# ReLU and squares of an MLP on ScalarE, four weight splits on VectorE, a bias page and later transposes

## The chip, the cores and the metric

The kernel runs on one core of one Trainium2 chip. The metric is the device time of one execution in microseconds, as the median over several runs. The profiled execution is a single one, and the durations below are from it.

## The reference

One encoder block: RMSNorm, one input projection, two groups of attention heads (A with a sliding window, ALiBi distance and sinks, B with a chunk band and relative positions), an output projection, then a squared-ReLU MLP, all in float32 on 1024 tokens of width 1024 with an inner width of 4096. What the change touches:

```python
scores = scores - slopes[:, :, None, None] * dist        # group A: slope 2^-(h+1) times |distance|
...
n2 = rms_norm(h, norm2_g[layer])
u = jnp.square(jax.nn.relu(jnp.einsum('bsd,df->bsf', n2, w_ff1[layer])))
h = h + jnp.einsum('bsf,fd->bsd', u, w_ff2[layer])
return rms_norm(h, final_norm_g)
```

## The kernel before

Every float32 operand of a large product is split into a high part (rounded to the matmul's operand type, a ScalarE copy) and a low part (`split_l`, L135: full minus high, on VectorE or GpSimd), and `mm3` (L129) issues three matmuls: high by high, high by low, low by high.

The work goes in stages: projections and attention of group A (pairs A0 to A3 of heads), of group B, the output projection (`out_proj_b`, tiles `op_B`, eight blocks of 128 tokens, `tb` 0 to 7), the first MLP product, the second one, the final norm. Both MLP products use a Strassen form: a 2 by 2 block product with seven products, numbered p = 1, 5, 6, 3, 7, 2, 4 in the order of execution. For each of eight column blocks n of the first product, `product1(n, p)` runs 24 matmuls into a PSUM tile `f1`. Its left operands `X{p}` come from the normalised tokens: transposes `tp` on TensorE, then copies (`F`) and sums (`S`) in `second_half` and `combined`, then split (`operand`, L848 and L135). Its weights: the blocks `w1` are loaded, combined into `T{n}_{p}` (VectorE, L902), split into `W{n}_{p}0` (high, ScalarE, L924) and `W{n}_{p}1` (low, L135, GpSimd before). `prepare1(n, p, at)` does that for the product at place `at` of `order1`, which begins (0,1), (0,2), (1,1), (0,5), (0,6), (0,3), (0,7), (1,5), (0,4).

After products 1, 5 and 6 ScalarE copies the PSUM tile into `kept` (`k`, L967). After 3, 7, 2 and 4 the result is complete but for a sum: `v` or `k` becomes the squared ReLU of PSUM plus the kept tile (L971 to L977), and is written to memory (`ud`) for the second product. After p = 4, four sums (L983 to L989) make the combined operands of the second product.

For the attention scores of group A, `exponentials` (L400) adds a bias to the scores, on VectorE, and takes the row minimum `nm`. The bias is the distance table `dist` times a power of two, made on GpSimd (L430) after a DMA (L429) at the first use of a pair of heads.

What sets the order: TensorE's instructions are issued in the order of the code. On the other engines a scheduler, which plays the program through, orders the instructions; each engine then works through its own list in that order and waits where an operand is late. DMAs are issued from SyncE's list (SP). `turns` holds pieces of work that `product1` and `out_proj_b` run between their matmuls, one entry at a time; an entry of `steps()` without work is an empty place. Tiles called `page` come from a pool of 35 buffers, `tst` from one of two, the PSUM tiles of the MLP from one of three.

Of the kernel before, what the change touches and what calls it, by code (L numbers as in the profile page):

```python
# [8 lines left out]
F32 = mybir.dt.float32  # L9
F32R = mybir.dt.float32r  # L10
AF = mybir.ActivationFunctionType
ALU = mybir.AluOpType
# [3 lines left out]
P = 128  # L16
# [29 lines left out]
def kernel(  # L46
# [26 lines left out]
    nc = tc.nc  # L73
# [10 lines left out]
    def page(shape, name, dt=F32R):  # L84
        return main.tile(shape, dt, tag="pg", bufs=NPAGES, name=name)
# [23 lines left out]
    def load(dst, src, mark=False):  # L109

        ins = nc.sync.dma_start(dst, src)
        if last_load[0] is not None:
            dep = mybir.DependencyInfo(mybir.DependencyClass.NoSync, mybir.DependencyReason.DATA)
            tc.add_manual_dep(ins.ins, last_load[0], dep, reason="program order")
        if mark:
            last_load[0] = ins.ins.name
# [17 lines left out]
    def split_l(engine, lo, full, hi):  # L134
        engine.tensor_tensor(lo, full, f(hi), ALU.subtract)  # L135

    def rstd(ss, n, width, name, r=None):

        if r is None:
            r = small.tile([P, width], F32, tag=f"rs{width}", name=f"r_{name}")  # L140
        u = small.tile([P, width], F32, tag=f"ru{width}", bufs=2, name=f"u_{name}")
        w = small.tile([P, width], F32, tag=f"rw{width}", bufs=2, name=f"w_{name}")
        q = small.tile([P, width], F32, tag=f"rq{width}", bufs=2, name=f"q_{name}")
        nc.scalar.activation(u, ss, AF.Sqrt, bias=eps4, scale=1.0 / (4 * n))
        nc.vector.tensor_scalar(w, ss, 1.0 / (4 * n), EPS / 4, ALU.mult, ALU.add)
        nc.vector.reciprocal(q, u)
        if width == 1:
            nc.vector.tensor_scalar(w, w, q, u, ALU.mult, ALU.add)
        else:
            nc.vector.tensor_tensor(w, w, q, ALU.mult)  # L150
            nc.vector.tensor_tensor(w, w, u, ALU.add)
        nc.vector.reciprocal(r, w)
        return r
# [51 lines left out]
    def load_xT(t, k):  # L205
        if k % 2 == 0:
            xs[t] = sp.tile([P, 2, HALF], F32, tag="xs", bufs=6, name=f"xs{t}{k // 2}")
        src = xs[t][:, k % 2]
        nc.sync.dma_start(src, xT_src[:, k, t * HALF : (t + 1) * HALF])
        gain = g1c[:, k : k + 1]  # L210
        hi, lo = (nT[t][hl][k // 2][:, k % 2] for hl in range(2))
        nc.scalar.activation(hi, src, AF.Copy, scale=gain)
        nc.vector.scalar_tensor_tensor(lo, src, gain, f(hi), ALU.mult, ALU.subtract)

    def token_scales(t):

        ss = small.tile([P, 4], F32, tag="ss4", name=f"ss1_{t}")
        for b in range(4):
            tb = 4 * t + b
            xr = sp.tile([P, D], F32, tag="xr", bufs=4, name=f"xr{tb}")  # L220
            load(xr, x[tb * P : (tb + 1) * P, :], True)
            nc.scalar.activation(xr, xr, AF.Square, accum_out=ss[:, b : b + 1])
        rstd(ss, D, 4, f"n1_{t}", r1[:, 4 * t : 4 * t + 4])
# [83 lines left out]
    dve, pool = nc.vector, nc.gpsimd  # L307
# [16 lines left out]
    for k in range(NK):  # L324
        load_xT(1, k)
    token_scales(1)
    load(psink, sinks.partition_broadcast(P))
    load(ogc, og)

# [33 lines left out]
    at = ap_.enter_context(tc.tile_pool(name="at", bufs=1, reuse_waits="tile"))  # L363
# [49 lines left out]
    class Pair:  # L413
# [5 lines left out]
            self.bias, self.out = [], {}  # L419

        def biases(self):
            if self.bias:
                return self.bias
            for s in range(2):
                h = 2 * self.j + s
                b = at.tile([P, 5 * P], F32, tag="bias", bufs=2, name=f"b_{self.kind}{h}")
                if self.kind == "A":
                    far = b[:, 2 * P : 4 * P]
                    nc.sync.dma_start(far, dist)  # L429
                    nc.gpsimd.tensor_scalar(b[:, : 2 * P], far, 2.0 ** -(h + 1), None, ALU.mult)  # L430
                else:
                    nc.sync.dma_start(b, relb[h])
                    nc.gpsimd.memset(b[:HD, 5 * P - HD :], NEG)
                    nc.gpsimd.memset(b[HD:, :HD], NEG)
                self.bias.append(b)
            return self.bias
# [219 lines left out]
    class Filler:  # L656
# [24 lines left out]
        def steps(self, n):  # L681
            self.due += n
            while self.due >= 1:
                self.due -= 1
                self.step()
# [90 lines left out]
    def flat(t):  # L776
        return t.rearrange("p a b -> p (a b)")
# [4 lines left out]
    def tst(shape, name):  # L782
        return main.tile(shape, F32, tag="tst", bufs=2, name=name)

    def pair_psum(name):
        return mps.tile([P, 2, HALF], F32, tag="ab", bufs=3, name=name)
# [94 lines left out]
    def steps(*works):  # L881
        turns.append([lambda f=f, a=a: f(*a) for f, *a in works])

    chores = {(0, 1): ((6, 0),), (0, 2): ((5, 1), (6, 1)), (1, 1): ((3, 0), (3, 1)), (0, 5): ((7, 0), (7, 1)), (0, 6): ((4, 0), (4, 1))}

# [34 lines left out]
    def split(full, name, engine, alloc):  # L922
        w = [alloc(f"{name}{hl}", hl) for hl in range(2)]
        nc.scalar.activation(w[0], full, AF.Copy)  # L924
        split_l(engine, w[1], full, w[0])
        return w

    wops, wsum = {}, {}

    def prepare1(n, p, at):  # L930
        if n >= NQ or (n, p) in wops:
            return
        made = wsum.setdefault(n, {})
        second = page2 if at < 2 or at > 4 else page1
        t = second_operands(
            lambda i, j: w1s[n, i, j], made, p, f"T{n}_{p}", dve, lambda name: second([P, 4, 2 * P], name)
        )
        wops[n, p] = split(t, f"W{n}_{p}", pool, lambda name, hl: (second if hl else page1)([P, 4, 2 * P], name, F32R))

    chains = {}  # L940

    def product1(n, p):
        a, c = chains.setdefault(n, [None, None])
        if p in (1, 5, 2):
            ps = pair_psum(f"f1_{n}_{p}")
            if p == 1:
                chains[n][0] = ps
            if p == 5:
                chains[n][1] = ps
        else:  # L950
            ps = c if p == 3 else a
        hi, lo = wops.pop((n, p))
        for u in range(2):
            cols = slice(u * P, (u + 1) * P)
            for k in range(4):
                x2 = [X[p][hl][k // 2][:, k % 2] for hl in range(2)]
                mm3(ps[:, u], (hi[:, k, cols], lo[:, k, cols]), x2, k == 0 and p in (1, 5, 2), k == 3, True)
                if k % 2:
                    turn()
        kept = saved.setdefault(n, {})  # L960
        ps = flat(ps)
        if p in (1, 5, 6):
            if p == 5 and n:
                kept[p] = tst([P, 2 * HALF], f"k{n}_{p}")
            else:
                kept[p] = page2([P, 2 * HALF], f"k{n}_{p}")
            nc.scalar.activation(kept[p], ps, AF.Copy)  # L967
            return
        v = tst([P, 2 * HALF], f"v{n}") if p == 4 else kept[{3: 6, 7: 5, 2: 1}[p]]
        if p == 7 or (n, p) == (0, 2):  # L970
            dve.tensor_tensor(v, ps, v, ALU.add)  # L971
            dve.scalar_tensor_tensor(v, v, 0.0, v, ALU.max, ALU.mult)
        else:
            if p != 4:
                dve.tensor_tensor(ps, ps, v, ALU.add)
            nc.scalar.activation(v, ps, AF.Relu)
            dve.tensor_tensor(v, ps, v, ALU.mult)  # L977
        if p != 4:
            put(n, {3: 2, 7: 4, 2: 1}[p], v)
            return  # L980

        u00, u01, u11, u10 = kept[1], kept[6], kept[5], v
        dve.tensor_tensor(u11, u10, u11, ALU.add)  # L983
        put(n, 5, u11)
        dve.tensor_tensor(u10, u00, u10, ALU.subtract)
        put(n, 7, u10)
        dve.tensor_tensor(u00, u11, u00, ALU.subtract)
        put(n, 6, u00)
        dve.tensor_tensor(u01, u01, u00, ALU.subtract)  # L989
        put(n, 3, u01)  # L990
# [17 lines left out]
    for tb in range(2, TB):  # L1008
        if tb in (3, 5):
            for d in range(2):  # L1010
                for g in range(2):
                    steps((first_half, d, tb // 4, g))
        if tb == 7:
            for g in range(2):
                steps((second_half, 0, g))
                steps()
        out_proj_b(tb, range(4))
        rows2(tb)
        if tb in (4, 5):
            prepare1(0, tb - 3, tb - 4)  # L1020
        if tb == 5:
            load1(1, ((0, 0),))
# [177 lines left out]
    g, p, n0 = order2[-GQ]  # L1200
# [57 lines left out]
```

## Time and profile before

| | us |
|---|---|
| median of 3 runs (lowest to highest) | 1082.0 (1081.73 to 1082.46) |
| profiled execution, its own time | 1082.73 |
| span of its profile | 1081.0 |
| TensorE busy | 1051.4 (97%) |
| VectorE busy | 754.9 (70%) |
| ScalarE busy | 535.9 (50%) |
| GpSimd busy | 436.7 (40%) |
| mean granted TensorE clock | 0.997 |

The page gives the busy time of each engine over the span. PE is TensorE's matmuls, PEld its weight loads, DVE is VectorE, ACT ScalarE, POOL GpSimd, SP SyncE. In rows of groups or of the timeline, `out<-in` names the tiles, the text behind it the shape, and what stands in brackets at the end is the idle time of the engine just before and the instruction that ended it. Buffer numbers are left out, so `W<-T,W` stands for any weight's split.

### The profile page before, as it was taken

The numbers are of one execution on the slowest core, as the hardware profiler recorded it, in microseconds if no ns is written. First come the engines' busy times: TensorE is split into PE (matmuls) and PEld (weight loads), VectorE is DVE, ScalarE is ACT, GpSimd is POOL, SyncE is SP. The second block draws the span as 40 slices with busy tenths as digits, with TensorE's granted clock in tenths as the row PEclk, the third lists the DMA queues.
The fourth block names the chain that finished last, engine by engine and source line by source line (L and its number), as shares of the span: only waits on it lengthen the run. The fifth ranks groups of instructions, "written<-read, shape, count | busy, mean of one in ns | idle before, by whom it ended". The sixth has DMA issues, their size and how long they took to land.

```text
span 1081.0 us, 14384 instructions
## 1 busy us (share of the span) xinstructions
PE 1051.4 (97%) x5040; PEld 873.0 (81%) x5040; DVE 754.9 (70%) x1162; ACT 535.9 (50%) x953; POOL 436.7 (40%) x320
## 2 busy tenths in 40 slices
PE   7999999999999999998999999999999999999997
PEld 6787878888888888877888888888788888888885
DVE  4577787667676765697755655656989776778667
ACT  7676765666574566654333333334423333333346
POOL 1376664343370243338453454445105024024025
PEclk9999999999999999999999999999999999999999
DMA  9945626353575342213454344516998535533004
GB/s 325 259 120 143 155 73 171 99 140 101 134 249 199 138 156 98 106 52 116 175 176 175 128 146 156 179 75 233 326 400 287 173 118 174 175 117 98 1 1 156
DMA packets 90584, 170.30 MB, mean 158 GB/s; under 512 B 7824, under 2 KB 43664, under 8 KB 90512
## 3 DMA queue, kind: packets, MB, share of 16 engines
q1 hardware_dynamic: 90368, 169.38, 47.6%
q8 instruction: 40, 0.66, 0.3%
q14 instruction: 32, 0.26, 0.1%
q10 hardware_dynamic: 144, 0.00, 0.0%
HBM read 105.39 MB, written 45.09 MB: 139 GB/s over the span
## 4 chain that ended last, share of the span: by engine, by line
PE 85%; DVE 7%; ACT 3%; issue 2%; DMA 2%; POOL 1%; SPq 1%; DVEq 0%; ACTq 0%
PE f L129 24%; PE f_a L129 16%; PE f_c L129 8%; PE op_B L129 4%; PE f_b L129 4%; PE op_A L129 4%; PE ip_qB L129 4%; PE ip_vB L129 3%; PE ip_kB L129 3%; PE av_B L129 3%; PE ip_qA L129 3%; PE S_B L129 2%; PE pt_B L132 2%; PE S_A L129 1%; PE av_A L129 1%
## 5 line engine op out<-in xcount | busy, mean ns | idle before, releaser
L129 PE MATMUL f<-X,W 128*128 128x512 f32 x1344 | 308.4, 391 | 6.5 <-POOL W L135 5.3
L129 PEld LDWEIGHTS f<-X,W 128*128 128x128 f32 x1344 | 252.9, 189 | 61.1 <-POOL W L135 6.1
L129 PE MATMUL f_a<-V,U 128*128 128x512 f32 x768 | 176.3, 389 | 0.7 <-DVE k L977 0.7
L135 POOL TENSOR_TENSOR U<-u,U 128x1024 fp32r<-128x1024 f32 x32 | 81.2, 2536 | 228.0 <-PE f_c L129 135.9
L129 PEld LDWEIGHTS f_a<-V,U 128*128 128x128 f32 x768 | 144.1, 188 | 31.0 <-issue 1.1
L135 POOL TENSOR_TENSOR W<-T,W 128x1024 fp32r<-128x1024 f32 x32 | 91.3, 2858 | 126.5 <-ACT W L924 126.5
L129 PE MATMUL f_c<-V,U 128*128 128x512 f32 x384 | 88.4, 389 | 0.0
L129 PEld LDWEIGHTS f_c<-V,U 128*128 128x128 f32 x384 | 72.1, 188 | 15.0
L924 ACT ACTIVATE V<-Z 128x1024 fp32r<-128x1024 f32 x32 | 33.9, 1060 | 94.6 <-PE f_a L129 44.6
L135 POOL TENSOR_TENSOR W<-w,W 128x1024 fp32r<-128x1024 f32 x24 | 61.0, 2544 | 35.1 <-ACT W L924 34.1
L135 DVE TENSOR_TENSOR V<-w,V 128x1024 fp32r<-128x1024 f32 x24 | 52.0, 2166 | 30.7 <-ACT V L924 30.2
L924 ACT ACTIVATE V<-w 128x1024 fp32r<-128x1024 f32 x24 | 25.4, 1059 | 81.2 <-issue 34.2
L924 ACT ACTIVATE U<-u 128x1024 fp32r<-128x1024 f32 x56 | 58.5, 1045 | 13.3 <-DVE Z L902 8.3
L924 ACT ACTIVATE W<-T 128x1024 fp32r<-128x1024 f32 x32 | 33.9, 1060 | 55.4 <-DVE T L902 28.6
L967 ACT ACTIVATE k<-f 128x1024 f32<-128x1024 f32 x24 | 24.6, 1026 | 65.6 <-PE f L129 65.6
L401 ACT ACTIVATE P_B<-P_B,nm_B 128x640 f32<-128x640 f32 (+2 forms) x64 | 44.3, 693 | 24.4 <-DVE nm_B L400 12.7
L129 PE MATMUL ip_kB<-nT,w_kB 128*128 128x512 f32 x192 | 51.5, 397 | 1.5 <-DVE T_A L135 0.8
L129 PE MATMUL op_A<-w_o,y 128*128 128x512 f32 x192 | 52.1, 397 | 0.5 <-DVE h L719 0.5
L135 DVE TENSOR_TENSOR V<-Z,V 128x1024 fp32r<-128x1024 f32 x32 | 46.3, 1448 | 8.4 <-ACT V L924 5.9
L129 PE MATMUL ip_vB<-nT,w_vB 128*128 128x512 f32 x192 | 51.9, 398 | 0.0
L129 PE MATMUL ip_qB<-nT,w_qB 128*128 128x512 f32 x192 | 51.5, 396 | 0.0
L135 DVE TENSOR_TENSOR T_B<-pt_B,T_B 128x512 fp32r<-128x512 f32 (+2 forms) x72 | 39.7, 552 | 16.7 <-ACT T_B L408 16.3
(211 smaller groups left out, 2024.7 us busy)
## 6 DMA issues: line engine op xcount, KB each, us to landing
w<-in_w_ff_dram SPq DMA_DIRECT2D x64, 512.0 KB, 4.7
u<-ud SPq DMA_DIRECT2D x56, 512.0 KB, 4.5
ud<-k SPq DMA_DIRECT2D x48, 512.0 KB, 3.0
KkB<-ts_kB SPq DMA_DIRECT2D x64, 128.0 KB, 2.3
yd<-y SPq DMA_DIRECT2D x14, 512.0 KB, 2.9
y<-yd SPq DMA_DIRECT2D x14, 512.0 KB, 6.4
xs<-in_xT_dram SPq DMA_DIRECT2D x16, 256.0 KB, 5.5
xr<-in_x_dram SPq DMA_DIRECT2D x8, 512.0 KB, 7.3
```

The source lines that it names most:

```text
L129: pe(nc.tensor.matmul(*args, **kw))
L132: pe(nc.tensor.transpose(*args))
L135: engine.tensor_tensor(lo, full, f(hi), ALU.subtract)
L401: nc.scalar.activation(pr[:, :n], pr[:, :n], AF.Exp, bias=nm, scale=-1.0, accum_out=sm)
L924: nc.scalar.activation(w[0], full, AF.Copy)
L967: nc.scalar.activation(kept[p], ps, AF.Copy)
```

## The change

It has four parts.

1. The two biases of the pair A0 are made in a page of their own, `b_A0`: one DMA of `dist` and two multiplies on GpSimd, written in the code ahead of the projections' steps. `Pair.biases` returns these for the pair A0.
2. The low parts of the weights at places 3 to 6 of `order1`, (0,5), (0,6), (0,3) and (0,7), are made on VectorE.
3. After products 3, 7 and 2, VectorE only adds PSUM and the kept tile into the kept tile; ScalarE does the ReLU and the square in place. After p = 4 ScalarE does the ReLU out of PSUM and the square in place.
4. At `tb` 7 the empty place comes ahead of `second_half`, so its transposes come one step of the output projection later.

```diff
@@ after token_scales(1)
+    fb = page([P, 3, 2 * P], "b_A0", F32)
+    load(fb[:, 2], dist)
+    first_bias = [fb[:, s] for s in range(2)]
+    for s in range(2):
+        pool.tensor_scalar(fb[:, s], fb[:, 2], 2.0 ** -(s + 1), None, ALU.mult)
     load(psink, sinks.partition_broadcast(P))
@@ Pair.biases
+            if self.kind == "A" and self.j == 0:
+                return first_bias
             if self.bias:
                 return self.bias
@@ prepare1
-        wops[n, p] = split(t, f"W{n}_{p}", pool, lambda name, hl: (second if hl else page1)([P, 4, 2 * P], name, F32R))
+        wops[n, p] = split(t, f"W{n}_{p}", dve if 2 < at < 7 else pool, lambda name, hl: (second if hl else page1)([P, 4, 2 * P], name, F32R))
@@ product1
-        if p == 7 or (n, p) == (0, 2):
+        if p == 4:
+            nc.scalar.activation(v, ps, AF.Relu)
+        else:
             dve.tensor_tensor(v, ps, v, ALU.add)
-            dve.scalar_tensor_tensor(v, v, 0.0, v, ALU.max, ALU.mult)
-        else:
-            if p != 4:
-                dve.tensor_tensor(ps, ps, v, ALU.add)
-            nc.scalar.activation(v, ps, AF.Relu)
-            dve.tensor_tensor(v, ps, v, ALU.mult)
+            nc.scalar.activation(v, v, AF.Relu)
+        nc.scalar.activation(v, v, AF.Square)
@@ tb == 7
             for g in range(2):
+                steps()
                 steps((second_half, 0, g))
-                steps()
```

The order on GpSimd at the start. Before, ahead of the first attention unit (`w1_vA`, `w1_qA1`, `w1_qA2` are low parts of projection weights, `P_A0` the normed exponentials of the first unit):

```order
L135 TENSOR_TENSOR w1_vA_239<-st_vA_237,w0_vA_238 128x256 x4
L135 TENSOR_TENSOR w1_qA1_476<-st_qA1_474,w0_qA1_475 128x256 x4
L367 MEMSET padF0_550 128x2x128
L369 MEMSET padL0_551 128x2x128
L369 MEMSET padL1_552 128x2x128
L430 TENSOR_SCALAR b_A0_568<-b_A0_568 128x256
L430 TENSOR_SCALAR b_A1_571<-b_A1_571 128x256
L135 TENSOR_TENSOR w1_qA2_580<-st_qA2_578,w0_qA2_579 128x256 x4
L505 TENSOR_SCALAR P_A0_0_0_563<-P_A0_0_0_563,rc_A0_0_561 128x256
```

GpSimd at the same place now:

```order
L135 TENSOR_TENSOR w1_vA_239<-st_vA_237,w0_vA_238 128x256 x4
L331 TENSOR_SCALAR b_A0_318<-b_A0_318 128x256 x2
L135 TENSOR_TENSOR w1_qA1_480<-st_qA1_478,w0_qA1_479 128x256 x4
L372 MEMSET padF0_554 128x2x128
L374 MEMSET padL0_555 128x2x128
L374 MEMSET padL1_556 128x2x128
L437 TENSOR_SCALAR b_A2_904<-b_A2_904 128x256
L437 TENSOR_SCALAR b_A3_907<-b_A3_907 128x256
L135 TENSOR_TENSOR w1_qA2_578<-st_qA2_576,w0_qA2_577 128x256 x4
L512 TENSOR_SCALAR P_A0_0_0_567<-P_A0_0_0_567,rc_A0_0_565 128x256
```

The first pair's two multiplies stand ahead of `w1_qA1`'s low part, and the place that they had holds those of the next pair (`b_A2`, `b_A3`, which stood twelve rows later). On SP the new DMA of `dist` stands behind the load of `st_qA1` and ahead of the DMAs that fill `KA`.

VectorE at the end of the output projection, before (`S0`, `S2` are the sums of `second_half` out of the transposes `tp_10`; L810 and L820 are the residual and the norm of the last token block):

```order
L868 TENSOR_TENSOR S0_0_5102<-tp_10_00_5112,F20_5101 128x2x256
L869 TENSOR_TENSOR S2_0_5104<-F00_4851,tp_10_00_5112 128x2x256
L868 TENSOR_TENSOR S0_1_5132<-tp_10_01_5142,F21_5131 128x2x256
L869 TENSOR_TENSOR S2_1_5134<-F01_4870,tp_10_01_5142 128x2x256
L810 SCALAR_TENSOR_TENSOR op_B_7_5094<-op_B_7_5094,rB_4674,h7_4522 128x1024
```

VectorE there now:

```order
L875 TENSOR_TENSOR S0_0_5106<-tp_10_00_5116,F20_5105 128x2x256
L876 TENSOR_TENSOR S2_0_5108<-F00_4849,tp_10_00_5116 128x2x256
L817 SCALAR_TENSOR_TENSOR op_B_7_5092<-op_B_7_5092,rB_4672,h7_4520 128x1024
L875 TENSOR_TENSOR S0_1_5136<-tp_10_01_5146,F21_5135 128x2x256
L876 TENSOR_TENSOR S2_1_5138<-F01_4868,tp_10_01_5146 128x2x256
```

The residual of the last block comes ahead of the second pair of sums. On TensorE each of the two groups of eight transposes stands behind six more matmuls of `op_B_7`; the second group now follows the last of them, directly ahead of product (0,1).

VectorE before, in the first products of the MLP, from the first transposes of the second token half on:

```order
L868 TENSOR_TENSOR S0_1_5132<-tp_10_11_5276,F21_5131 128x2x256
L869 TENSOR_TENSOR S2_1_5134<-F01_4870,tp_10_11_5276 128x2x256
L135 TENSOR_TENSOR X610_5225<-S1_0_5103,X600_5223 128x2x256
L876 TENSOR_TENSOR S1_1_5133<-S0_1_5132,F01_4870 128x2x256 x2
L971 TENSOR_TENSOR k0_1_5220<-f1_0_2_5238,k0_1_5220 128x1024
L135 TENSOR_TENSOR X610_5225<-S1_0_5103,X600_5223 128x2x256
L135 TENSOR_TENSOR X511_5184<-S0_1_5132,X501_5182 128x2x256
L135 TENSOR_TENSOR X611_5226<-S1_1_5133,X601_5224 128x2x256
L902 TENSOR_TENSOR T0_6_5232<-w1_0_11_4801,T0_5_5189 128x1024
L135 TENSOR_TENSOR X611_5226<-S1_1_5133,X601_5224 128x2x256
L972 SCALAR_TENSOR_TENSOR k0_1_5220<-k0_1_5220 128x1024
L878 TENSOR_TENSOR S3_0_5105<-F10_4885,S1_0_5103 128x2x256 x2
```

VectorE there now:

```order
L875 TENSOR_TENSOR S0_1_5136<-tp_10_11_5274,F21_5135 128x2x256
L876 TENSOR_TENSOR S2_1_5138<-F01_4868,tp_10_11_5274 128x2x256
L983 TENSOR_TENSOR k0_1_5218<-f1_0_2_5236,k0_1_5218 128x1024
L135 TENSOR_TENSOR X611_5224<-S1_1_5137,X601_5222 128x2x256
L912 TENSOR_TENSOR T0_6_5230<-w1_0_11_4799,T0_5_5187 128x1024
L883 TENSOR_TENSOR S1_1_5137<-S0_1_5136,F01_4868 128x2x256
L135 TENSOR_TENSOR X511_5182<-S0_1_5136,X501_5180 128x2x256
L135 TENSOR_TENSOR W0_61_5233<-T0_6_5230,W0_60_5232 128x1024
L135 TENSOR_TENSOR X611_5224<-S1_1_5137,X601_5222 128x2x256
L135 TENSOR_TENSOR W0_31_5302<-w1_0_11_4799,W0_30_5301 128x1024
L885 TENSOR_TENSOR S3_0_5109<-F10_4883,S1_0_5107 128x2x256 x2
```

`W0_61` and `W0_31` have come in, `W0_51` stands a few rows earlier, right behind the sums out of `tp_10_10`, and `W0_71` later, behind the eight splits of `X3` and `X7`; the squared ReLU (L972) is gone, and the add of product (0,2) (L971, now L983) stands one place behind the same two sums. On ScalarE a ReLU and a square of `k0_1` stand between the high part of `X501` and that of `W0_6`.

More of the change, by code (lines that the diff above doesn't have):

```diff
@@ L882, in steps @@
         turns.append([lambda f=f, a=a: f(*a) for f, *a in works])
-    chores = {(0, 1): ((6, 0),), (0, 2): ((5, 1), (6, 1)), (1, 1): ((3, 0), (3, 1)), (0, 5): ((7, 0), (7, 1)), (0, 6): ((4, 0), (4, 1))}
+    chores = {
+        (0, 1): ((6, 0),), (0, 2): ((5, 1), (6, 1)), (1, 1): ((3, 0), (3, 1)), (0, 5): ((7, 0), (7, 1)),
+        (0, 6): ((4, 0), (4, 1)),
+    }
     w1s = {}
```

## The prediction

> **What bounds the kernel now.** I read the busy times of the page first, then what TensorE waited for, then its idle time by place, and then the timeline at the places where it waits.
>
> ```profile
> span 1081.0 us, 14384 instructions
> PE 1051.4 (97%) x5040; PEld 873.0 (81%) x5040; DVE 754.9 (70%) x1162; ACT 535.9 (50%) x953; POOL 436.7 (40%) x320
> ```
>
> TensorE is busy in 97% of the span, so 29.6 us of it are all that any reordering of other engines can win, as long as TensorE's own matmuls stay the same, and here they do. So the question is which of its waits the change takes away, and whether it makes new ones. The waits of TensorE:
>
> ```profile
> PE f L129 <- POOL W L135: 5.3, 2, 3.4
> PE S_A L129 <- DVE nm_A L400: 2.6, 2, 2.0
> PE f L129 <- DVE k L971: 1.0, 1, 1.0
> PE tp L132 <- ACT F L865: 0.7, 1, 0.7
> PE f_a L129 <- DVE k L977: 0.7, 1, 0.7
> PE tp L132 <- DVE S L869: 0.5, 1, 0.5
> PE f L129 <- DVE X L135: 0.2, 1, 0.2
> ```
>
> These seven sum to 11.0 us (total, times, longest). The change touches the releaser of each. The stretches of 40 us say where they lie; the columns are the busy time of PE, PEld, DVE, ACT and POOL, then the granted clock:
>
> ```profile
> 0.00:40.00 40.00, 34.11 (x146) 26.96 (x147) 19.57 (x43) 28.52 (x51) 6.54 (x16) 1.00 0.93 302
> 440.00:480.00 40.00, 36.88 (x176) 29.86 (x175) 34.46 (x43) 19.69 (x30) 11.61 (x4) 1.00 0.26 92
> 480.00:520.00 40.00, 36.42 (x152) 29.36 (x151) 30.71 (x28) 19.40 (x24) 25.99 (x9) 0.96 0.34 119
> 520.00:560.00 40.00, 40.00 (x178) 33.11 (x177) 23.44 (x17) 14.05 (x14) 21.30 (x9) 1.00 0.49 170
> 760.00:800.00 40.00, 38.30 (x169) 31.07 (x168) 38.17 (x31) 16.01 (x16) 5.89 (x2) 1.00 1.00 370
> ```
>
> The entry of the first MLP product (440 to 520) loses 6.7 us of TensorE and part of the clock; 520:560 loses nothing, and it stands for the steady part of that product; the passage from the first to the second product (760:800) loses 1.7.
>
> **Part 1, the bias page.** At the start of attention:
>
> ```profile
> 25.86 0.38 SPq L111 DMA_DIRECT2D st_qA<-in_w_in_dram  x1
> 29.90 6.41 SPq L261 DMA_DIRECT2D KA<-ts_kA  x8
> 36.99 2.82 POOL L135 TENSOR_TENSOR w_qA<-st_qA,w_qA 128x256 fp32r<-128x256 f32 x4 [17.07 <-ACT w_qA L172]
> 45.45 1.67 POOL L430 TENSOR_SCALAR b_A<-b_A 128x256 f32<-128x256 f32 x2 [4.89 <-issue]
> 43.29 0.68 DVE L135 TENSOR_TENSOR ts_qA<-ts_qA 128x512 fp32r<-128x512 f32 x1
> 46.34 0.35 DVE L400 CUSTOM_DVE_ANT_0 P_A<-S_A,b_A,nsink 128x128 f32<-128x128 f32 x1 [2.36 <-POOL b_A L430]
> 42.96 2.23 PE L129 MATMUL ip_qA<-nT,w_qA 128*128 128x512 f32 x9
> 47.16 0.74 PE L129 MATMUL S_A<-KA,QA 128*128 128x256 f32 x4 [1.97 <-DVE nm_A L400]
> ```
>
> The chain is GpSimd's bias multiply, VectorE's `exponentials`, TensorE's next scores. The new DMA is issued behind `st_qA`, in SP's idle time between 26.24 and 29.90, and moves 128 KB: at the 302 GB/s of the first 40 us that is 0.4 us for whatever lies behind it, the fills of `KA` and `QA` included. GpSimd is idle for 17.07 us ahead of 36.99, and the page is filled in that time or a little after, so the multiplies (2 in 1.67 us) are done by about 38 instead of 47.1. If the DMA lands as late as `st_qA`, which it follows, they delay `w_qA`'s low part by at most 1.7 us, of the 3.1 that lie between its end (39.81) and the `ip_qA` at 42.96. VectorE can then start `exponentials` at 43.97, where `ts_qA` ends, instead of 46.34, that is 2.37 earlier, and the scores at 47.16 start when TensorE gets there, at 45.19: 1.97 us. GpSimd's place at 45.45 is not empty now: the next pair's two multiplies stand there, with `w_qA2`'s low part and the norm of `P_A` behind them, so what hangs on the norm does not come 2 us earlier. I take 1.8 of the 1.97; ends: -0.4 (nothing won, and the DMA delays the scores), and 2.6 (both waits of this kind gone).
>
> **Parts 2 and 4, the entry of the MLP.** The timeline there:
>
> ```profile
> 448.65 0.66 PE L132 MATMUL tp<-ident,n 128*128 128x128 f32 x4 [0.69 <-ACT F L865]
> 455.44 2.40 POOL L135 TENSOR_TENSOR W<-w,W 128x1024 fp32r<-128x1024 f32 x1 [15.70 <-ACT W L924]
> 455.64 2.74 DVE L876 TENSOR_TENSOR S<-S,F 128x512 f32<-128x512 f32 x1
> 461.84 0.68 DVE L876 TENSOR_TENSOR S<-S,F 128x512 f32<-128x512 f32 x1
> 473.62 3.94 POOL L135 TENSOR_TENSOR W<-T,W 128x1024 fp32r<-128x1024 f32 x1 [8.84 <-ACT W L924]
> 477.53 2.85 POOL L135 TENSOR_TENSOR W<-w,W 128x1024 fp32r<-128x1024 f32 x1
> 477.62 5.53 PE L129 MATMUL f<-X,W 128*128 128x512 f32 x23 [1.85 <-POOL W L135]
> 481.45 1.21 DVE L902 TENSOR_TENSOR T<-w,w 128x1024 f32<-128x1024 f32 x1
> 484.18 1.05 ACT L924 ACTIVATE W<-T 128x1024 fp32r<-128x1024 f32 x1
> 485.31 14.00 POOL L135 TENSOR_TENSOR W<-T,W 128x1024 fp32r<-128x1024 f32 x3 [4.93 <-ACT W L924]
> 492.68 3.71 PE L129 MATMUL f<-X,W 128*128 128x512 f32 x9 [3.40 <-POOL W L135]
> ```
>
> Products (0,6) and (0,7) wait for their low parts on GpSimd: 1.85 and 3.40 us. A lone split on GpSimd takes 2.40, the one for (0,6) took 3.94, and the three from 485.31 took 14.00. The same sum `S` on VectorE takes 0.68 alone and 2.74 beside GpSimd's split: the two engines hold each other up when both read two operands from SBUF. The Trainium skill states this as a rule ("SBUF — State Buffer", section "SBUF: two separate sides"): whichever starts first holds the shared ports for its whole instruction, and the other blocks. By that rule one split that stays on GpSimd could also stop VectorE's splits for its 2.40 us, and the trace agrees in size, since 2.74 less 0.68 is 2.06.
>
> A split of that shape on VectorE costs what the other two-operand instructions of 128x1024 do there, 1.21 (481.45). Four are 4.8 us more for VectorE, whose 34.46 busy of 440:480 hold delays such as that 2.06, which go, since GpSimd has nothing there between `W1_11` and `W1_51`. Out of the same stretch go the squared ReLU of (0,2) and, of (0,5)+(0,3), one multiply, 1.2 each. The low part of (0,6) is ready about 1.2 us after its high part instead of 3.94, that of (0,7) likewise instead of 8.5 us after 484.18 (its wait ended at 492.68).
>
> The low parts now stand in VectorE's row, so what lies behind them waits: `W0_51` delays `X510` and what follows by 1.2, and it must itself wait for ScalarE's high part. I worked VectorE's list through in its new order with these durations. The wait for the transposes at 461 (0.5) stays. `X511`, behind a larger part of the list, comes 0.4 to 0.8 us after product (0,5) wants it. `W0_61` and `W0_31` are ready about 2 us ahead of (0,6), `W0_71` about 1.5 ahead of (0,7), and GpSimd's first split, `W1_51`, about 1 to 4 us ahead of (1,5).
>
> The slow clock is a term of its own: 23 matmuls from 477.62 took 5.53 (0.24 each), the 9 from 492.68 took 3.71; 9 at 0.24 are 2.2, so the wait of 3.40 cost some 1.5 more behind it. The windows' clock is 0.96 there and 1.00 behind the 1.85 wait. The Trainium skill ("TensorE: Matmul & The Clock Gate", section "What's actually happening") has the clock halved after an idle window of about 3.4 us; by that rule any wait that stays shorter costs no clock, and the trace agrees (3.40 here, none after 1.85).
>
> Transposes: the wait of 0.69 at 448.65 is for ScalarE's `F` copy of the group before, which shares two buffers. With six more matmuls between the groups' inputs and the transposes it goes; the last block's residual (L810) starts earlier too, as its matmuls no longer stand behind eight transposes.
>
> Sum of what is lost here now: 0.7 + 0.5 + 1.85 + 0.2 + 3.40 + 1.5 = 8.15, and some smaller waits between matmuls (about 1.1 by their starts, which the rows do not list as waits) make 9.3. What stays: 0.5 for the transposes and 0.6 for `X511`. I take 8.2. Ends: 4 (only the half, see the rivals) and 9.3 (all).
>
> **Part 3, ReLU and squares.** Between the products:
>
> ```profile
> 758.08 1.21 DVE L135 TENSOR_TENSOR V<-Z,V 128x1024 fp32r<-128x1024 f32 x1
> 759.21 1.21 DVE L977 TENSOR_TENSOR k<-f,k 128x1024 f32<-128x1024 f32 x1
> 760.34 1.21 DVE L971 TENSOR_TENSOR k<-f,k 128x1024 f32<-128x1024 f32 x1
> 761.70 5.72 PE L129 MATMUL f<-X,W 128*128 128x512 f32 x24 [1.02 <-DVE k L971]
> 769.46 1.22 DVE L977 TENSOR_TENSOR k<-f,k 128x1024 f32<-128x1024 f32 x1
> 770.83 7.54 PE L129 MATMUL f_a<-V,U 128*128 128x512 f32 x32 [0.69 <-DVE k L977]
> L967 ACT ACTIVATE k<-f 128x1024 f32<-128x1024 f32 x24 | 24.6, 1026 | 65.6 <-PE f L129 65.6
> ```
>
> VectorE loses 32 instructions in all (four per column block), some 39 us at 1.21. ScalarE gains as many ReLUs and squares: 41 more instructions, at 1.03 (L967, out of PSUM) to 1.05 (484.18, out of SBUF), 43 us over the first product. In the steady part ScalarE goes from 14 of 40 us to about 19, VectorE from 23 to about 19, and TensorE has no wait to lose, since the weights are made several products ahead; I cost this at nothing. The cover is that lead. If it were gone, a pair of 2.1 us in ScalarE's list ahead of a high part would be seen, up to 23 times. The ReLU now waits for VectorE's add with the next weights' high part behind it on ScalarE; the add waits for nothing but its product and VectorE's list, so that wait is short where VectorE is not full.
>
> At the passage the multiply at 759.21 stands ahead of the add at 760.34, for which the last product waits 1.02; without it the add starts 1.2 us earlier, and the wait goes. The PSUM tile for the second wait (0.69, for the multiply at 769.46) is now free after the add alone, some 4 us earlier. Both are 1.7, and 2.0 with the slower starts around them. VectorE is full here (38.17 of 40), so what it sheds comes at the right place. Ends: 0.5 (other VectorE work takes the place) and 2.0. Behind that, TensorE's next waits are those at the start of attention that nothing here touches.
>
> **The sum.** 1.8 + 8.2 + 2.0 = 12.0 against the profiled execution's 1082.73: 1070.7. The median of the runs stands 0.7 below that execution, so the median should be 1070.0. Ends added: 14 (1068) and 4 (1078); all low ends together are unlikely.
>
> **The rivals.**
> - *VectorE becomes the bound of the entry.* It speaks for this that it is busy 34.46 of 40 there and gets four splits more, each behind a ScalarE copy; against it that half of its load there was waiting for GpSimd. Then `X511`, `X310` or `W0_71` come late by 1 to 2 us each, the gain is 4 of 9.3, and the time is 1074.
> - *The front pays nothing.* The DMA of the bias queues behind `st_qA` in a stretch with DMA share 0.93, and `KA` and `QA` behind it; without part 1, 1071.8.
> - *Slower: ScalarE's list.* It runs in order, and a ReLU that waits for VectorE's add holds up the high part behind it. The price is the add's delay plus 2.1 us, at 23 places. From the point where a weight's high part has less lead than that, TensorE waits at each: 1 us each would be +23 - 12, so 1093. Against it: TensorE is full in 520:560, and ScalarE is busy 14.05 of 40 there.
> - *No net change*: the waits for `W` become waits for `X` of the same length, as VectorE's list gets longer at the same place; 1081, if parts 1 and 3 pay only what that costs.
>
> **How the numbers follow.** The forecast has 0.62, VectorE as the bound 0.16, the front without gain 0.12, no net change 0.05, slower 0.05. About 0.2% (2 us) is what this kernel's measurement can tell from no change. The first three are faster by far more, so faster 0.91, same 0.04, slower 0.05. The range goes from 1067.0, a little below all upper ends, to 1075.0, which takes in the rival with VectorE.
>
> **What would show it.** In the changed profile: `S_A` has no wait of 2 us for `nm_A`, and the first bias multiplies end before 40. No wait for `W` on GpSimd above 1 us near 475 and 490, a clock of 1.00 in 480:520, and TensorE above 38.5 busy in both windows of the entry. No wait for `k` near 760 and 770. 520:760 still full, ScalarE near 19 of 40. The forecast is wrong if VectorE shows a chain of splits with TensorE behind it around 468, or if waits for ScalarE's `W` appear in the steady part.

## The result, and the profile after

The changed kernel takes 1072.55 us (median of 4 runs, 1071.56 to 1074.59) against 1081.9 before; the ratio is 0.9915, interval [0.9898, 0.9932]. The profiled execution took 1074.59, the longest of its four. The page of the changed kernel begins:

```profile
span 1072.5 us, 14369 instructions
PE 1050.7 (98%) x5040; PEld 874.1 (82%) x5040; DVE 706.3 (66%) x1134; ACT 579.5 (54%) x994; POOL 416.7 (39%) x316
```

TensorE's own time is nearly the same (1051.4 before); the span is 8.5 us shorter, 7.8 of them idle time of TensorE. Of the seven kinds of waits that the prediction listed, one is left:

```profile
PE S_A L129 <- DVE nm_A L405: 3.3, 2, 1.9
```

It has grown, from 2.6 to 3.3. The stretches (busy PE, PEld, DVE, ACT, POOL, then clock) say where the time came from. The first line is 40:80 of the kernel before, the others are of the changed kernel:

```profile
40.00:80.00 40.00, 37.42 (x205) 31.43 (x203) 27.52 (x83) 27.82 (x76) 25.79 (x32) 1.00 0.67 172
40.00:80.00 40.00, 36.52 (x187) 30.22 (x186) 27.16 (x76) 25.25 (x72) 24.39 (x31) 0.96 0.66 168
440.00:480.00 40.00, 39.95 (x194) 33.11 (x193) 34.40 (x50) 25.06 (x39) 5.51 (x4) 1.00 0.27 92
480.00:520.00 40.00, 40.00 (x179) 33.11 (x178) 28.61 (x27) 25.80 (x31) 20.25 (x9) 1.00 0.43 145
520.00:560.00 40.00, 40.00 (x178) 33.15 (x177) 17.28 (x13) 20.65 (x20) 21.08 (x9) 1.00 0.49 171
760.00:800.00 40.00, 40.00 (x178) 33.14 (x177) 34.37 (x27) 15.94 (x17) 4.81 (x2) 1.00 0.98 378
```

The entry (440 to 520) and the passage (760 to 800) are full. Counted by the starts of the matmuls (for each matmul, the distance to the one before it, less the usual distance for that shape), TensorE's loss in 440:520 went from 9.9 to 0.5 us and in 760:800 from 2.2 to none. In 40:80 it rose from 3.5 to 6.4, and the clock fell to 0.96: the start of attention gave some of it back.

The entry in detail, on the timeline of the changed kernel:

```profile
464.19 1.21 DVE L135 TENSOR_TENSOR W<-T,W 128x1024 fp32r<-128x1024 f32 x1
464.41 27.84 PE L129 MATMUL f<-X,W 128*128 128x512 f32 x120
473.32 1.23 DVE L135 TENSOR_TENSOR W<-T,W 128x1024 fp32r<-128x1024 f32 x1 [0.23 <-ACT W L934]
475.06 1.22 DVE L135 TENSOR_TENSOR W<-w,W 128x1024 fp32r<-128x1024 f32 x1
489.12 2.47 POOL L135 TENSOR_TENSOR W<-T,W 128x1024 fp32r<-128x1024 f32 x1 [29.54 <-ACT W L934]
```

VectorE's splits take 1.21 to 1.23, GpSimd's next one, for (1,5), takes 2.47, and 120 matmuls run without a wait. The start of attention:

```profile
43.49 0.35 DVE L405 CUSTOM_DVE_ANT_0 P_A<-S_A,b_A,nsink 128x128 f32<-128x128 f32 x1
44.62 0.64 PE L129 MATMUL S_A<-KA,QA 128*128 128x256 f32 x4
52.12 0.69 DVE L249 SCALAR_TENSOR_TENSOR ts_qA<-ip_qA,R 128x512 f32<-128x512 f32 x1 [1.15 <-DMA QA<-ts_qA]
52.84 0.64 ACT L252 ACTIVATE ts_qA<-ts_qA 128x512 fp32r<-128x512 f32 x1 [1.75 <-DMA QA<-ts_qA]
58.84 0.74 PE L129 MATMUL S_A<-KA,QA 128*128 128x256 f32 x4 [1.89 <-DVE nm_A L405]
59.42 1.97 PE L129 MATMUL ip_qA<-nT,w_qA 128*128 128x512 f32 x6
71.85 1.95 DVE L512 TENSOR_SCALAR P_A<-P_A,rc_A 128x256 f32<-128x256 f32 x2
71.88 1.29 POOL L135 TENSOR_TENSOR ts_qA<-ts_qA 128x512 fp32r<-128x512 f32 x1 [6.42 <-DVE rc_A L509]
75.04 1.53 DVE L636 SCALAR_TENSOR_TENSOR y<-Y,ogc,y 128x512 fp32r<-128x512 f32 x1
77.30 0.75 PE L129 MATMUL S_A<-KA,QqA 128*128 128x256 f32 x4 [1.43 <-DVE nm_A L405]
```

The first exponentials start at 43.49 instead of 46.34 and the score at 47.16 is now at 44.62, with no wait. But VectorE's `ts_qA` at 52.12 waits 1.15 (before, it began at 52.36 without a wait), the score at 58.84 waits 1.89 where that at 59.53 waited 0.61, the matmuls behind it run slower (6 in 1.97 instead of 1.53), and there is a new wait of 1.43 at 77.30. Near 72, VectorE's norm of `P_A` (1.95) and GpSimd's split of `ts_qA` run at the same time. Theory A of the first experiments is read off these rows: the page's gain is taken back by the wait for a buffer, by half clock, and by VectorE and GpSimd holding each other up near 72.

### The profile page after: what moved, and what is told of

It is laid out like the page before. It is cut to its first block, busy times and chain, and to the rows that moved or that the text cites. A ratio compares the mean times of both kernels' runs of the same rounds, so it can differ in the third digit from the quotient of the medians.

```text
span 1072.5 us, 14369 instructions
## 1 busy us (share of the span) xinstructions
PE 1050.7 (98%) x5040; PEld 874.1 (82%) x5040; DVE 706.3 (66%) x1134; ACT 579.5 (54%) x994; POOL 416.7 (39%) x316
## 4 chain that ended last, share of the span: by engine, by line
PE 86%; DVE 6%; issue 3%; DMA 2%; ACT 2%; SPq 1%; POOL 1%; DVEq 0%; ACTq 0%; POOLq 0%
PE f L129 27%; PE f_a L129 16%; PE f_c L129 8%; PE op_B L129 4%; PE f_b L129 4%; PE op_A L129 4%; PE ip_qB L129 4%; PE ip_kB L129 3%; PE ip_vB L129 3%; PE av_B L129 3%; PE pt_B L132 2%; PE S_B L129 2%; PE ip_qA L129 2%; PE S_A L129 1%; PE av_A L129 1%
## 5 line engine op out<-in xcount | busy, mean ns | idle before, releaser
L135 POOL TENSOR_TENSOR W<-T,W 128x1024 fp32r<-128x1024 f32 x29 | 75.7, 2613 | 139.1 <-ACT W L934 139.1
L983 DVE TENSOR_TENSOR k<-f,k 128x1024 f32<-128x1024 f32 x24 | 29.3, 1221 | 61.9 <-PE f L129 61.9
L135 POOL TENSOR_TENSOR W<-w,W 128x1024 fp32r<-128x1024 f32 x23 | 57.3, 2492 | 32.2 <-ACT W L934 32.0
L135 DVE TENSOR_TENSOR V<-w,V 128x1024 fp32r<-128x1024 f32 x24 | 47.2, 1972 | 27.4 <-ACT V L934 27.4
L129 PE MATMUL ip_qA<-nT,w_qA 128*128 128x512 f32 x192 | 51.3, 406 | 0.0
```

Of the source, the lines that this page charges most:

```text
L129: pe(nc.tensor.matmul(*args, **kw))
```

## The experiments

Times are medians, ratios (with their 95% intervals) are to the kernel before, run beside it, and "loss" is TensorE's loss by starts of matmuls in the profiled execution.

**Without the bias page** (parts 2, 3 and 4):

```diff
-    fb = page([P, 3, 2 * P], "b_A0", F32)
...
-            if self.kind == "A" and self.j == 0:
-                return first_bias
```

> The changed kernel without the bias page (parts 2, 3 and 4 alone). Theory A (the bias page costs: its win is taken back by a second score wait, by half clock behind that, and by VectorE waiting for GpSimd near 72): 1070.2, that is 1082.0 less the 9.5 of the entry and the 2.2 of the passage, and the two waits for nm_A are those of before (2.0 and 0.6). Rival B (the bias page wins 1.8 as forecast, and the rest of the change is worth less than the trace says): 1074.3, slower than the changed kernel.

1070.87, 0.9893 [0.9877, 0.9909]. The waits for `nm_A` are those of before (2.0 and 0.8 by starts), the loss in 40:80 is 3.4, in 440:520 0.4. Rival B would have it slower than the change, which it is not. On VectorE near 70 the same two instructions as above, in this kernel:

```profile
69.87 0.75 DVE L505 TENSOR_SCALAR P_A<-P_A,rc_A 128x256 f32<-128x256 f32 x2
71.86 0.99 DVE L629 SCALAR_TENSOR_TENSOR y<-Y,ogc,y 128x512 fp32r<-128x512 f32 x1
```

**The bias page alone** (before with the `fb` lines and the return in `Pair.biases`).

> The kernel before with the bias page alone. Theory A: slower than before by 1 to 3, 1083 to 1085, with a score wait of about 2 near 57 and one of about 1.5 near 76. Rival B: 1080.2, the score wait near 45 gone and no new one.

1083.07, 1.0004 [0.9993, 1.0015]: no gain and no loss that can be measured. Rival B's 1080.2 is out; the difference of 0.4 us is below the 1 to 3 of Theory A, though the waits are as it says: none at 45, and by starts 2.16 ahead of the score at 58.9 and 1.59 ahead of that at 75.75. The loss in 40:80 is 5.0 against 3.5, and in this execution without half clock.

**The next pair's biases put back** to where they stood before:

```diff
-                    nc.sync.dma_start(far, dist)
+                    ins = nc.sync.dma_start(far, dist)
+                    if self.j == 1:
+                        dep = mybir.DependencyInfo(mybir.DependencyClass.NoSync, mybir.DependencyReason.DATA)
+                        tc.add_manual_dep(ins.ins, placed["qA1", 1], dep, reason="program order")
```

> The changed kernel with the next pair's two bias DMAs and multiplies put back to the place that they had before (behind the fills of QqA from ts_qA1_1). Theory A: GpSimd's ts_qA split near 72 comes behind a multiply again and no longer meets VectorE's norm, so the wait for nm_A near 76 (1.4 to 1.6) goes, 1.5 to 2 less than the changed kernel: 1070.5 to 1071. Rival C (the wait near 76 comes from the later arrival of everything behind the half clock near 60): it stays, same time as the changed kernel, 1072.5.

1072.42, 0.9907 [0.9890, 0.9923], the changed kernel's time. The wait near 76 stayed (1.60). GpSimd's row in this kernel shows why this edit does not decide it:

```profile
67.43 1.79 POOL L443 TENSOR_SCALAR b_A<-b_A 128x256 f32<-128x256 f32 x2 [0.94 <-DMA b_A<-in_dist_dram]
72.15 1.29 POOL L135 TENSOR_TENSOR ts_qA<-ts_qA 128x512 fp32r<-128x512 f32 x1 [2.93 <-DVE rc_A L515]
72.12 1.95 DVE L518 TENSOR_SCALAR P_A<-P_A,rc_A 128x256 f32<-128x256 f32 x2
```

The multiplies were done by 69.2, before the split could start, so the split still began with VectorE's norm. In the kernel before, the second multiply came late and held GpSimd from 71.01 to 71.98, until the norm was over:

```profile
70.92 0.75 DVE L505 TENSOR_SCALAR P_A<-P_A,rc_A 128x256 f32<-128x256 f32 x2
71.01 0.97 POOL L430 TENSOR_SCALAR b_A<-b_A 128x256 f32<-128x256 f32 x1 [1.34 <-DVE rc_A L502]
```

Theory A's expectation for this kernel was a miss, because the edit did not bring that order back. Rival C does not hold either: the kernel with the bias page alone has this wait with no half clock ahead of it.

**The staging tile of `ts_qA1` in a page:**

```diff
-        elif name == "vA":
+        elif name == "vA" or (name, t) == ("qA1", 0):
             st = page([P, 2, HALF], f"ts_{name}_{t}")
```

> The changed kernel with the staging tile of ts_qA1's first half in a page instead of the third turn of the two tst buffers. Theory A (VectorE's list stands still until 52.1 since ts_qA1 waits for a buffer that the KA or QA fills must leave, which come at the same time as before): the wait at 52.1 goes, the score at 58.8 starts 0.7 or more earlier, the wait of 1.9 there falls to about 1 and no half clock follows; 1070 to 1071.5. Rival D (ts_qA1 waits for its projection on TensorE, not for a buffer): nothing moves, 1072.5.

1070.57, 0.9893 [0.9877, 0.9909]. VectorE and TensorE in this kernel:

```profile
50.40 0.68 DVE L249 SCALAR_TENSOR_TENSOR ts_qA<-ip_qA,R 128x512 f32<-128x512 f32 x1
57.13 0.74 PE L129 MATMUL S_A<-KA,QA 128*128 128x256 f32 x4 [0.85 <-DVE nm_A L405]
```

`ts_qA` starts at 50.40 without a wait, the score at 57.13 instead of 58.84, and its wait is 0.85 instead of 1.89. So the buffer, which a DMA had to leave, was what took the first wait's gain; Rival D is out. The second wait stayed at 1.59 by starts.

**The changed kernel once more:**

> The changed kernel once more, beside the others of this call. Both theories: 1072 to 1073, with waits of about 2.1 near 57 and 1.6 near 76 for nm_A. Theory A adds that the stretch of half clock behind the first of them comes in some executions and not in others, so that the profile shows either 0.96 or 1.00 in 40:80.

1072.58, 0.9902 [0.9886, 0.9917]. The same place of this execution:

```profile
40.00:80.00 40.00, 36.60 (x197) 30.45 (x196) 28.50 (x81) 26.20 (x75) 25.00 (x32) 1.00 0.67 172
58.85 0.75 PE L129 MATMUL S_A<-KA,QA 128*128 128x256 f32 x4 [1.90 <-DVE nm_A L405]
59.43 1.54 PE L129 MATMUL ip_qA<-nT,w_qA 128*128 128x512 f32 x6
```

The wait is the same 1.90, but 6 matmuls take 1.54 and the clock is 1.00: the half clock, which costs about 1.6 us (a loss of 6.4 against 4.8), comes in some executions only. The last section shows what it depends on.

**The page, and GpSimd's split behind VectorE's norm** (an added wait; the split then stands behind GpSimd's own norms):

```diff
+        if (name, t) == ("qA2", 0):
+            dep = mybir.DependencyInfo(mybir.DependencyClass.Sync, mybir.DependencyReason.DATA)
+            tc.add_manual_dep(lo.ins, normed["A0_6"], dep, reason="after norm")
```

> The changed kernel with the staging tile in a page, and with GpSimd's split of ts_qA2's first half made to wait for VectorE's norm of the unit A0_6 (it then stands behind GpSimd's own norms). Theory A (the wait near 76 is VectorE's norm, 1.95 instead of 0.75 for two, and its y, 1.5 instead of 1.0, both beside a two-operand instruction of GpSimd): the norm takes 0.75 to 0.9, the wait falls below 0.5, and the time is 1069.2, 1.3 less than with the page alone. Rival E (the wait is the exponentials' own chain over TensorE and ScalarE): 1.6 stays, 1070.5.

1070.46, 0.9883 [0.9868, 0.9898].

```profile
68.58 0.84 DVE L518 TENSOR_SCALAR P_A<-P_A,rc_A 128x256 f32<-128x256 f32 x2
70.60 1.30 POOL L255 TENSOR_TENSOR ts_qA<-ts_qA 128x512 fp32r<-128x512 f32 x1
70.66 1.79 DVE L644 SCALAR_TENSOR_TENSOR y<-Y,ogc,y 128x512 fp32r<-128x512 f32 x1
```

The norm is back to 0.84, but the split now meets `y`, which takes 1.79 instead of 0.99. The wait fell from 1.59 to 0.74 by starts, where below 0.5 was expected, and the time by less than can be told. That speaks for Theory A and against Rival E, as far as it goes.

**The page, and that split on VectorE:**

```diff
+        low_engine = nc.vector if (name, t) == ("qA2", 0) else low_engine
         split_l(low_engine, st[:, 1], f(st[:, 1]), st[:, 0])
```

> The changed kernel with the staging tile in a page, and the low part of ts_qA2's first half on VectorE instead of GpSimd; VectorE's list then also has y behind the first exponentials of the next pair. Theory A (the wait near 72 to 76 is VectorE beside GpSimd's two-operand split): the norm takes 0.75 to 0.9, no split of GpSimd is near, and y no longer stands ahead of the exponentials; the wait of 1.6 with the page alone falls below 0.3, TensorE's loss in 40:80 below 2, and the time is 1069.0. Rival E (the wait is a chain over TensorE and ScalarE, or VectorE with 0.69 more is late anyway): above 1.0 stays, 1070.5 or more.

1069.35, 0.9878 [0.9855, 0.9901], the lowest of all kernels here. Its stretch, its waits for the scores, and VectorE's two instructions:

```profile
40.00:80.00 40.00, 39.04 (x215) 33.03 (x214) 29.87 (x90) 28.60 (x80) 25.35 (x31) 1.00 0.70 184
PE S_A L129 <- DVE nm_A L406: 1.0, 1, 1.0
69.15 1.02 DVE L513 TENSOR_SCALAR P_A<-P_A,rc_A 128x256 f32<-128x256 f32 x2
71.94 0.75 DVE L637 SCALAR_TENSOR_TENSOR y<-Y,ogc,y 128x512 fp32r<-128x512 f32 x1
```

The second wait is gone, and the loss in 40:80 is 1.8 (before: 3.5, changed: 6.4 and 4.8, without the page: 3.4). The norm, at 1.02, is a little over the 0.75 to 0.9 expected. Two things changed here, the engine of the split and the place of `y`; which of them did more stays open. The time is 1.2 below that with the staging tile alone, which is not more than the intervals can tell.

**Part 2 alone** (the four low parts on VectorE):

> The kernel before with part 2 alone, four low parts on VectorE. Theory A (GpSimd's splits, with the port they share with VectorE, are nearly the whole loss of the entry): the waits for W of 1.85 and 3.40 and the half clock go, 1075.2. Rival F (VectorE, which still has its multiplies, becomes late itself): half of that stays as waits for X or W made by VectorE, 1078.5.

1076.65, 0.9941 [0.9918, 0.9964], between the two expectations. The waits for GpSimd and the half clock are gone, but a new one came in 480:520. VectorE became late itself, as Rival F has it, though with `k` and not with `X` or `W`:

```profile
491.75 1.21 DVE L977 TENSOR_TENSOR k<-f,k 128x1024 f32<-128x1024 f32 x1
493.10 1.17 PE L129 MATMUL f<-X,W 128*128 128x512 f32 x4 [1.97 <-DVE k L977]
```

Product (1,5) waits for a PSUM tile that the old multiply still reads, and that multiply stands in VectorE's list behind the added work. The loss of 440:520 is 3.9, instead of 9.9.

**Part 4 alone** (the later transposes):

> The kernel before with part 4 alone, the transposes one step later. Theory A (what TensorE wins at the transposes it waits longer for the low parts on GpSimd, which come when they came): the wait of 0.85 near 448 goes, the waits for W grow by nearly as much, 1081.5 to 1082. Rival G (GpSimd's low parts come earlier too, since the last residual does): 1081.1 or less.

1082.35, 1.0005 [0.9993, 1.0017]. What TensorE waits for in the entry:

```profile
PE f L129 <- POOL W L135: 5.3, 2, 4.7
PE f L129 <- DVE X L135: 1.0, 1, 1.0
```

Both waits at the transposes went. The waits for GpSimd's low parts still sum to 5.3 (the one before (0,7) grew from 3.4 to 4.7, that before (0,6) fell from 1.85 to 0.6), and a wait of 1.0 for `X` came where 0.2 was. The loss of 440:520 is 9.1 instead of 9.9. Alone the part wins nothing that the times show, as Theory A said.

**Part 3 alone** (ReLU and squares):

> The kernel before with part 3 alone, ReLU and squares on ScalarE. Theory A: the two waits of the passage (1.18 and 0.79) go, the steady part stays full, and the entry keeps its waits for GpSimd's low parts, so 1080.0. Rival H (VectorE, freed of three instructions in the entry, makes T earlier, and GpSimd's splits meet it less): the waits for W in the entry shrink too, 1077 to 1079.

1079.12, 0.9972 [0.9959, 0.9985]. The passage is full, which is 2.2 by starts. The wait for GpSimd before (0,6) fell to 0.9 by starts from 2.0, so Rival H has a share of it; that before (0,7) stayed, and in the profiled execution half clock lasted longer there (clock 0.91 in 480:520, 0.96 before), so that its loss in 440:520 is 9.8, no better than 9.9:

```profile
PE f L129 <- POOL W L135: 4.1, 2, 3.4
```

**Parts 2 and 3 without 1 and 4:**

> Parts 2 and 3 without the later transposes and without the bias page. Theory A (with the low parts on VectorE the wait of 2.1 at 490 for the multiply of k goes too, and what stays are the two waits at the transposes, 0.85 and 0.67): 1.2 above the kernel without the bias page, 1072.0. Rival I (the later transposes win nothing by themselves): 1070.9.

1071.47, 0.9903 [0.9876, 0.9929]. In 440:520 only the two waits at the transposes are left (0.85 and 0.67 by starts), so with parts 2 and 3 together both the waits for GpSimd and the one for the multiply are gone. The loss there is 1.7, against 0.4 with part 4 as well (without the bias page). The times differ by 0.6 (1070.87 there), halfway between Theory A's 1.2 and Rival I's nothing, and not more than the runs can tell.

## Why the prediction was right or wrong

The direction and the range held, 1072.55 in 1067.0 to 1075.0; the gain was 9.35 us where 12.0 was forecast. The mechanism held for the MLP and failed for the bias page. By starts, the entry gave 1.2 and the passage 0.2 more than forecast, and the bias page 3.1 to 4.7 less, so the total is as near as it is partly by luck: the entry's surplus hides part of the page's miss.

- **Entry.** Forecast 8.2 of 9.3, measured 9.4 by starts. The mechanism held: the splits took 1.21 on VectorE, the half clock behind the wait of 3.40 went with it, and `X511` was not late by the 0.4 to 0.8 that I took off (0.2 by starts at (0,5)). The wait at the transposes, which I had left in, went too. The rival with VectorE as the bound fell: it is busy 34.40 in 440:480 as before (34.46), with three of the four splits more, and 28.61 in 480:520 (30.71 before), with the fourth. But it falls only with part 3: splits and squares need each other in the entry. By starts its loss of 9.9 goes to 3.9 with the splits alone, which end in the wait for the multiply, to 9.8 with the squares alone, which leave GpSimd's waits, and to 1.7 with both. In whole times they bring 5.5 and 2.9 alone (2.2 of the 2.9 is the passage), and 10.6 together.
- **Passage.** Forecast 2.0, measured 2.2 by starts. Part 3 alone takes both waits away, as worked out.
- **Steady part.** Forecast nothing, measured nothing: 520:560 is full with ScalarE at 20.65 and VectorE at 17.28. ScalarE's list did not hold up the weights, so the slower rival fell. The instructions, on ScalarE in 520:760 of the changed kernel, cost what was taken:

```profile
L984 ACT ACTIVATE k<-k 128x1024 f32<-128x1024 f32 x20 | 21.2, 1062 | 8.6 <-DVE k L983 8.5
```

- **Bias page.** This is the step that failed: "I take 1.8 of the 1.97; ends: -0.4 ... and 2.6". The first wait did go, as worked out (the multiplies were done at 37.9, the exponentials started 2.85 earlier and the score 2.5, of which 0.4 is the earlier start of all work there). But I looked only at what hangs on GpSimd's norm, and not at VectorE's own next instruction in order: `ts_qA` stood ahead of the second unit's last exponentials and needed a buffer that a DMA, a fill of `QA`, frees at 52, however early VectorE gets there. There the wait of 1.15 took back what was won, and the score at 58.84 was 0.69 earlier than before instead of 2.5. That the page's own DMA delays those fills, as the rival on the front had it, is likely but not shown: from the first score to their issue it is 6.0 to 6.9 us in the seven profiles with the page and 5.4 to 6.2 in the six without, 0.6 more on average. Then came GpSimd's split beside VectorE's norm, 1.59 by starts, since in the kernel before a late multiply had kept the two apart. "GpSimd's place at 45.45 is not empty now" was noted; that its place at 71 becomes empty was not. By starts the term is a loss of 1.3 us without half clock and 2.9 with it, where a gain of 1.8 was put. In the times it is less certain: the page alone is 0.04% slower, with 0.07% faster inside its interval, and without it the change is about 1.7 us lower than with it, with intervals that overlap. With the buffer and the split out of the way, the loss in 40:80 is 1.8 against 3.4 without the page, so the gain that I put was there to be had.
- **Clock.** The rule "any wait that stays shorter costs no clock" was drawn from the Trainium skill ("TensorE: Matmul & The Clock Gate", section "What's actually happening") and one row, and two traces contradict it: half clock behind a wait of 1.89. The section also says that the window runs free and does not start with the work. The traces agree (last section), and this is why two other traces with the same wait show no half clock: there the wait is spread over two windows.

The rival "the front pays nothing" (1071.8) was nearest to the measured time, with 0.12 of the chance, but that is luck in part: the front lost time instead of paying nothing, and its reason, fills behind the new DMA, would be about 0.6 us of that. Without the page the kernel took 1070.87, below the rival's time, since the entry gave more than forecast.

## What to carry to other kernels

A wait removed early in a chain is worth what the next instruction in the same engine's list can use: read each in-order list past the removed wait until something that does not move, above all a buffer that a DMA must free. An instruction that seems to have cost only time (a late multiply on GpSimd) may have kept two engines off a shared resource, so see what meets what once it is gone. Edits that are worth little alone can be worth more together: the splits alone ended in the multiply's wait, which the other part took out.

## What the runs showed of the hardware that was not expected

Half clock came behind a wait of 1.89 us, in two of the four profiled executions that have this wait (the changed kernel and the one with the biases put back; not in the changed kernel's second profile nor with the bias page alone). The clock column, read over short stretches, shows why. In all 13 traces the clock changes only at whole multiples of 3.413 us from the first change to full clock, and half clock lasts 3.41 us (once, with part 3 alone, two such windows). In the changed kernel the windows end at 60.36 and 63.77; in its second profile at 57.37, 60.78 and 64.19 (columns as above; what the PE column lacks of the length is TensorE's idle time):

```profile
56.94:60.36 3.42, 1.53 (x10) 1.35 (x10) 3.19 (x10) 1.30 (x5) 3.42 (x5) 1.00 0.26 64
60.36:63.77 3.41, 3.41 (x10) 2.67 (x9) 1.77 (x8) 2.50 (x9) 1.57 (x3) 0.50 0.58 161
53.95:57.37 3.42, 3.00 (x17) 2.23 (x15) 1.55 (x5) 2.59 (x8) 2.59 (x4) 1.00 1.00 226
57.37:60.78 3.41, 1.93 (x10) 1.71 (x11) 3.17 (x11) 1.72 (x7) 3.01 (x4) 1.00 0.24 69
60.78:64.19 3.41, 3.41 (x21) 2.84 (x19) 2.04 (x7) 2.70 (x8) 2.14 (x2) 1.00 0.59 158
```

In the first execution the whole wait, 1.89, falls into one window, and the next window has half clock. In the second one the wait is split, 0.42 and 1.48, and none follows. The other two agree: 1.99 in one window with the biases put back, 0.9 and 1.0 in two with the bias page alone. Of all windows at full clock in the 13 traces, up to 1040 us, the six with 1.89 us of idle time or more were followed by half clock, and none of those with 1.70 or less was. No window here lies between the two. Half clock for 3.41 us costs TensorE half of that, 1.7, which agrees with the 1.6 by starts.

VectorE's norm of two tiles, which reads one tile from SBUF and a column of factors, took 0.75 beside GpSimd's bias multiply, 0.84 and 1.02 beside GpSimd's norms, and 1.95 beside GpSimd's two-operand split. So what GpSimd runs matters more than that it runs. And the prediction was too narrow in saying that the two hold each other up when both read two operands from SBUF: here VectorE's instruction reads one.
